# A fixed instruction order on three engines for the attention block of the second mixer

## The chip, the cores and the metric

The kernel runs on one core of a Trainium2 chip. The metric is the device time of one execution in microseconds (us), as a median over runs. The core's engines work side by side, each through its own list of instructions in order: PE (TensorE: matrix products and transposes), DVE (VectorE), ACT (ScalarE), POOL (GpSimd) and SP (SyncE, which issues the transfers). An instruction that needs the result of another engine waits for a semaphore, and everything behind it on its own engine waits with it.

## The reference, cut to what matters

The reference is one step of a two-layer trunk for 128 prompt tokens and 256 latent tokens of width 1024: in each layer a half SwiGLU, a mixer, and a half SwiGLU. The mixer of layer 1 holds two attentions with 8 heads of 64 each: a sliding window with a sink (SWA), and a two-dimensional neighbourhood with a relative bias (NA). The outputs of both are concatenated and multiplied by one weight matrix:

```python
def odd_mixer_latent(h, params, cache):
    w_in, w_out, rpb, sink = params
    kc_ctx, vc_ctx, kd_ctx, vd_ctx = cache
    L = h.shape[1]
    qc, kc, vc, qd, kd, vd = odd_project(h, w_in)
    yc = na_latent(qc, kc, vc, kc_ctx.astype(kc.dtype), vc_ctx.astype(vc.dtype), rpb)
    cos, sin = axial_rope(L, qd.dtype)
    yd = swa_latent(apply_rope(qd, cos, sin), apply_rope(kd, cos, sin), vd,
                    kd_ctx.astype(kd.dtype), vd_ctx.astype(vd.dtype), sink)
    return jnp.concatenate([yc, yd], axis=-1) @ w_out, ()
...
    # in both, for each block of 128 queries:
    p = jax.nn.softmax(scores, axis=-1)      # SWA: a sink column, a band mask; NA: scores + bias
    o = p @ v
```

## The kernel before, in words

**Two halves of each number.** Every product with a weight is made of three matmuls on halves of both factors: `whi` and `wlo` are the rounded weight and what rounding left of it (`hh`, `hl` and `ydh`, `ydl` are the same for activations). ACT rounds (`whi`, line 121), and DVE or POOL subtracts (`wlo`, line 122). A transfer brings a block `raw`; in the attention block all of `wlo` is POOL's (`ws.every = 1`).

**The attention block** (`mixer1`, lines 1135 to 1155) has 24 items: 8 pairs of heads, four of SWA and then four of NA, and for each pair three blocks T of 128 tokens in the order T = 1, 2, 0. T = 1 and 2 are latent tokens (384 keys, two turned tiles), and T = 0 is the prompt (128 keys, one turned tile). For an item, PE makes the scores `S` of both heads (lines 658 and 659, with a mask in SWA, line 707), DVE writes the sink column (709) or adds the bias (711) and takes the maximum (628), ACT makes the exponentials `E` (630), DVE takes the reciprocal of their sum (631) and scales `E` (633), PE transposes `E` into `pt` (719), ACT copies it to `PT` (723, 725), PE multiplies it with the values (732), ACT rounds the result (`ydh`, `ych`, 637) and DVE subtracts (`ydl`, `ycl`, 638). The tile `pt` has two banks. A T = 1 or 2 item takes both, and the value product writes into the first, so the next item's transposes wait for the `ydl` of the one before.

**The turn of item n** is, in the program: its transposes; some fill; the scores and probabilities of item n+2; its value products and split; some more fill. A fill is a unit of three weight matmuls of a list with 64 units: the queries of the four NA pairs (`fm`, after which ACT and DVE make the stack `qn`, lines 647 and 648), then the output product of SWA (`mo`). `FILL = ((1, 2), (1, 2), (0, 1))` says how many units come at the two places for n mod 3. "Slot" below is a place at which a new block of weights is split, which falls into a fill about every 3.5 turns.

**The key stacks of NA** (`na_keys`, for each pair two half-stacks of 64 rows by 512): ACT rounds (`kdn`, 653), POOL copies the rounded half to the other partitions (1103), DVE subtracts (`kln`, 655).

**What sets the order.** Only PE is bound to the program's order there (`in_order`). ACT and DVE take their order from the framework's scheduler, which moves instructions by its own model; POOL and SP too.

Of the kernel before, what the change touches and what calls it, by code (L numbers as in the profile page):

```python
# [13 lines left out]
P = 128  # L14
# [122 lines left out]
def body(ctx, tc, d):  # L137
# [483 lines left out]

    def soft(pool, S, n, nk):

        nm = pool.tile([P, 2], F32, tag="nm", name="nm", bufs=3)
        sm = pool.tile([P, 2], F32, tag="sm", name="sm", bufs=3)
        E = work(pool, 2 * n, "E", 770, 2).rearrange("p (a n) -> p a n", a=2)
        for j in range(2):
            nc.vector.tensor_reduce(nm[:, j:j + 1], S[j][:, :n], axis=AX.X, op=ALU.max, negate=True)
        for j in range(2):
            nc.scalar.activation(E[:, j], S[j][:, :n], AF.Exp, bias=nm[:, j:j + 1], accum_out=sm[:, j:j + 1])  # L630
        nc.vector.reciprocal(sm, sm)
        for j in range(2):
            nc.vector.tensor_scalar(E[:, j, :nk], E[:, j, :nk], sm[:, j:j + 1], None, op0=ALU.mult)
        return E

# [7 lines left out]

    def stack_q(q, p, j):
# [16 lines left out]
    class Stacks:  # L661
# [20 lines left out]
        def keys(self, src, T):  # L682
# [12 lines left out]
    def attn(pool, i, T, scores, vals, Y, mask=None, sink=None, bias=None):  # L695

        nb = len(vals)
        nk = nb * P
        st = {}

        def probabilities():
            S = [bank("S", "S") for _ in range(2)]
            for j in range(2):
                scores(S[j], i, j, T, mask is not None and T > 0)
                if mask is not None and T > 0:
                    o = P if T == 2 else 2 * P
                    nc.tensor.matmul(S[j][:, o:o + P], identb, mask[:, T - 1], start=False, stop=True)
                if sink is not None:
                    nc.vector.tensor_copy(S[j][:, nk:nk + 1], sink(i, j))
                if bias is not None and T > 0:  # L710
                    nc.vector.tensor_tensor(S[j][:, 0:2 * P], S[j][:, 0:2 * P], bias(T)[:, j], op=ALU.add)
            st["E"] = soft(pool, S, nk + (sink is not None), nk)

        def turned():
            pt = [bank("pt", "pt") for _ in range(1 + (nb > 1))]
            for j in range(2):
                for k in range(nb):
                    o = (k if nb > 1 else j) * P
                    nc.tensor.transpose(pt[j * (nb > 1)][:, o:o + P], st["E"][:, j, k * P:(k + 1) * P], ident)  # L719
            PT = st["PT"] = work(pool, 2 * nk, "PT", 768, 1).rearrange("p (a n) -> p a n", a=2)  # L720
# [5 lines left out]
            st["y"] = pt[0][:, NT:NT + P]  # L726

        def output():
            y, PT = st["y"], st["PT"]
            for k in range(nb):  # L730
                for j in range(2):
                    nc.tensor.matmul(y[64 * j:64 * j + 64, :], vals[k](j), PT[:, j, k * P:(k + 1) * P],  # L732
                                     start=k == 0, stop=k == nb - 1)
            split_y(y, Y[i][0][:, T * P:(T + 1) * P], Y[i][1][:, T * P:(T + 1) * P])

        return probabilities, turned, output
# [3 lines left out]
    def finish(left=0):  # L740

        while len(tails) > left:
            for step in tails.pop(0):
                step()

    def attn_pair(pool, i, scores, vf, vctx, Y, mask=None, sink=None, bias=None):
        for T in (1, 2):
            vals = [lambda j: vf(j, 1), lambda j: vf(j, 2)]
            yield attn(pool, i, T, scores, vals + [vctx] if bias else [vctx] + vals, Y, mask, sink, bias)
        yield attn(pool, i, 0, scores, [lambda j: vf(j, 0)], Y, None, sink)  # L750
# [25 lines left out]
    def mixer0():  # L776
        with ExitStack() as es:
# [135 lines left out]
            def attn_a(i):  # L913
                for first, *rest in attn_pair(mp, i, sk.scores, vf, lambda j: vctx[:, 64 * j:64 * j + 64], YA):
                    first()
                    tails.append(rest)
# [134 lines left out]
    def mixer1():  # L1051
        with ExitStack() as es:
# [45 lines left out]
            def na_keys(i):  # L1098
                rpb = mp.tile([P, 2, 2, 256], F32, tag="rpb", name="rpb", bufs=2)
                nc.sync.dma_start(rpb, d["rpb"][:, i])  # L1100
                kl, kd = kln[i % 2], mp.tile([P, 2, 512], F32R, tag="kdn", name="kdn", bufs=2)
                for j in range(2):
                    stack_k(kd[:, j], kl[:, j], kc[:, i], j, lambda d, s: nc.gpsimd.tensor_copy(d, s))
                kn[i] = kd, kl, rpb
# [30 lines left out]
            items = [it for i in range(4) for it in swa(i)] + [it for i in range(4) for it in na(i)]  # L1135
            ws.every = 1
# [207 lines left out]
```

## Time and profile before

| | us |
|---|---|
| median of 3 runs | 1545.02 (1544.58 to 1545.17) |
| the profiled execution | 1544.98 |
| its span in the trace | 1543.3 |
| mean granted clock of PE | 0.993 of full speed |
| PE busy | 1507.2, 98% of the span |
| DVE busy | 1130.4, 73% |
| ACT busy | 681.2, 44% |
| POOL busy | 138.8, 9% |
| attention block, 1139.10 to 1237.34 | 98.24, of which PE busy 90.11 |

Busy times overlap, so they do not add up to the span. A row of a timeline gives the start in us from the span's start, the duration, the engine, the line, the operation and what it writes and reads; a bracket at its end says how long the engine had idled and on whom it waited. Neighbours that are alike are joined into one row (x2), whose duration then runs from the first one's start to the last one's end.

### The profile page before, as it was taken

To read this page: it belongs to the slowest core of one execution; us is meant where nothing else is said; L and a number is where in the kernel's file an instruction comes from. 1 tells how busy PE (TensorE), PEld (TensorE's weight loads), DVE (VectorE), ACT (ScalarE), POOL (GpSimd) and SP (SyncE) were. 2 spreads that over 40 slices of the span, in tenths; PEclk is the share of its full clock that TensorE was granted. 3 is DMA by queue.
4 is the path that set the end of the run, shared out by engine and by line. 5 is a ranking of instruction groups with operands and counts; after the bars stand their busy time and mean duration, and the time that the engine had idled before them with its cause. 6 is when DMAs were issued, how large, how long until landed. Compare 5 with 4: busy or idle time off the path is not lost.

```text
span 1543.3 us, 23024 instructions
## 1 busy us (share of the span) xinstructions
PE 1507.2 (98%) x8888; PEld 1450.6 (94%) x8888; DVE 1130.4 (73%) x2158; ACT 681.2 (44%) x1318; POOL 138.8 (9%) x120
## 2 busy tenths in 40 slices
PE   7999999998999999999999999999999999999997
PEld 5999999996888999999999999999887799999997
DVE  3799999976666899999449899954857777444333
ACT  4643333366654643333345433333667555333321
POOL 2100000113011200000000000001222220000010
PEclk9999999999999999999999999999999999999999
DMA  9555666543002546666354566634431223333331
GB/s 379 225 191 215 249 252 238 213 145 111 28 28 96 217 149 255 235 235 218 112 209 172 214 229 263 240 118 155 143 120 42 69 101 119 137 110 137 119 127 41
DMA packets 40654, 256.91 MB, mean 166 GB/s; under 512 B 4448, under 2 KB 8544, under 8 KB 11232
## 3 DMA queue, kind: packets, MB, share of 16 engines
q1 hardware_dynamic: 40544, 255.43, 46.0%
q8 instruction: 70, 1.15, 0.3%
q14 instruction: 40, 0.33, 0.1%
HBM read 252.52 MB, written 2.89 MB: 166 GB/s over the span
## 4 chain that ended last, share of the span: by engine, by line
PE 94%; DVE 3%; issue 1%; ACT 1%; DMA 0%; POOL 0%; POOLq 0%; SPq 0%; DVEq 0%; ACTq 0%
PE gu L378 16%; PE gu L379 16%; PE gu L380 16%; PE fo L380 8%; PE fo L378 8%; PE fo L379 8%; PE tm L589 2%; PE tm L590 2%; PE pt L732 2%; PE tm L591 2%; PE mo L378 2%; PE mo L380 1%; PE mo L379 1%; PE pt L719 1%; PE fm L378 1%
## 5 line engine op out<-in xcount | busy, mean ns | idle before, releaser
L121 ACT ACTIVATE whi<-raw 128x1024 fp32r<-128x1024 f32 (+2 forms) x378 | 344.6, 927 | 630.5 <-issue 204.7
L122 DVE TENSOR_TENSOR wlo<-raw,whi 128x1024 fp32r<-128x1024 f32 (+2 forms) x335 | 372.4, 1118 | 195.9 <-ACT whi L121 194.7
L378 PE MATMUL gu<-mh,whi 128*128 128x384 f32 x976 | 329.1, 338 | 1.4 <-ACT whi L121 1.4
L379 PE MATMUL gu<-ml,whi 128*128 128x384 f32 x976 | 329.0, 337 | 0.0
L380 PE MATMUL gu<-mh,wlo 128*128 128x384 f32 x976 | 328.2, 337 | 0.0
L256 DVE SCALAR_TENSOR_TENSOR junk<-adaw,cond 128x1024 bf16<-128x1024 f32 x256 | 313.1, 1223 | 2.1 <-DMA adaw<-ada 0.4
L378 PE MATMUL fo<-gh,whi 128*128 128x384 f32 x704 | 235.1, 334 | 0.0
L379 PE MATMUL fo<-gl,whi 128*128 128x384 f32 x704 | 235.1, 334 | 0.0
L380 PE MATMUL fo<-gh,wlo 128*128 128x384 f32 x704 | 235.1, 334 | 0.0
L378 PEld LDWEIGHTS gu<-mh,whi 128*128 128x128 f32 x976 | 183.8, 188 | 2.3 <-ACT whi L121 2.3
L380 PEld LDWEIGHTS gu<-mh,wlo 128*128 128x128 f32 x976 | 183.7, 188 | 0.0
L379 PEld LDWEIGHTS gu<-ml,whi 128*128 128x128 f32 x976 | 183.6, 188 | 0.0
L378 PE MATMUL gu<-hh,whi 128*128 128x386 f32 x432 | 149.4, 346 | 1.4 <-ACT hh L350 1.4
L379 PE MATMUL gu<-hl,whi 128*128 128x386 f32 x432 | 147.1, 341 | 1.5 <-DVE hl L351 1.5
L380 PE MATMUL gu<-hh,wlo 128*128 128x386 f32 x432 | 146.2, 340 | 0.0
L292 POOL TENSOR_TENSOR ssq<-ssq,sq 128x384 f32<-128x384 f32 x43 | 49.0, 1139 | 1055.7 <-issue 798.1
L378 PEld LDWEIGHTS fo<-gh,whi 128*128 128x128 f32 x704 | 132.1, 188 | 0.0
L379 PEld LDWEIGHTS fo<-gl,whi 128*128 128x128 f32 x704 | 132.1, 188 | 0.0
L380 PEld LDWEIGHTS fo<-gh,wlo 128*128 128x128 f32 x704 | 132.1, 188 | 0.0
L378 PEld LDWEIGHTS gu<-hh,whi 128*128 128x128 f32 x432 | 81.8, 189 | 4.8 <-issue 2.9
L379 PEld LDWEIGHTS gu<-hl,whi 128*128 128x128 f32 x432 | 81.8, 189 | 2.1 <-DVE hl L351 2.1
L380 PEld LDWEIGHTS gu<-hh,wlo 128*128 128x128 f32 x432 | 81.8, 190 | 0.0
(286 smaller groups left out, 2069.2 us busy)
## 6 DMA issues: line engine op xcount, KB each, us to landing
adaw<-ada SPq DMA_DIRECT2D x64, 1024.0 KB, 5.4
raw<-f2i SPq DMA_DIRECT2D x44, 1024.0 KB, 4.7
raw<-f1i SPq DMA_DIRECT2D x43, 1024.0 KB, 4.8
raw<-f1o SPq DMA_DIRECT2D x22, 1024.0 KB, 4.8
raw<-f2o SPq DMA_DIRECT2D x22, 1024.0 KB, 4.7
raw<-mo SPq DMA_DIRECT2D x8, 1024.0 KB, 4.9
aw<-aw SPq DMA_DIRECT2D x7, 1024.0 KB, 7.7
raw<-mic SPq DMA_DIRECT2D x6, 1024.0 KB, 4.8
```

The costliest lines, as they stand in the source:

```text
L121: i1 = nc.scalar.activation(hi[:, a:e], src[:, a:e], AF.Copy)
L122: i2 = (self.nc.gpsimd if j % self.every == 0 else self.sub).tensor_tensor(lo[:, a:e], src[:, a:e], hi[:, a:e].bitcast(F32), op=ALU.subtract)
L256: iv = nc.vector.scalar_tensor_tensor(junk, t, 1.0, ada_state["cond"][:, g], op0=ALU.mult, op1=ALU.mult, accum_out=MOD[l][:, j, g, c:c + 1])
L292: nc.gpsimd.tensor_tensor(ssq_t["t"], ssq_t["t"], sq, op=ALU.add)
L378: nc.tensor.matmul(out, wh, xh, start=first, stop=False)
L379: nc.tensor.matmul(out, wh, xl, start=False, stop=False)
L380: return nc.tensor.matmul(out, wl, xh, start=False, stop=last)
L589: nc.tensor.matmul(out[T], hh, wh, start=k == 0, stop=False)
L590: nc.tensor.matmul(out[T], hh, wl, start=False, stop=False)
L591: nc.tensor.matmul(out[T], hl, wh, start=False, stop=k == DC - 1)
L719: nc.tensor.transpose(pt[j * (nb > 1)][:, o:o + P], st["E"][:, j, k * P:(k + 1) * P], ident)
L732: nc.tensor.matmul(y[64 * j:64 * j + 64, :], vals[k](j), PT[:, j, k * P:(k + 1) * P], start=k == 0, stop=k == nb - 1)
```

## The change

The closure `attn` becomes a class `Item` with the steps `scores`, `exps`, `scaled`, `turned`, `values` and `split`, and the block binds ACT and DVE to the program's order too. A turn is now: transposes; fill; scores of n+2 (both heads' products, then both masks, then for each head sink or bias and maximum); value products of n; exponential of n+2's head 0; split of n; exponential of head 1; fill; reciprocal and scaling of n+2; and in eight named turns one half-stack of NA keys. The half-stack's subtraction goes from DVE to POOL, and its rounding for the first two pairs from ACT to DVE. The first mixer uses the same class with its steps in the old order.

```diff
-    def stack_k(kd, kl, k, j, dup):
+    def stack_k(kd, kl, k, j, dup, sub, rounded=None):
         b, o = halves(j)
-        nc.scalar.activation(kd[b], k[b], AF.Copy)
+        (rounded or copy)(kd[b], k[b])
         dup(kd[o], kd[b].bitcast(F32))
-        nc.vector.tensor_tensor(kl[b], k[b], kd[b].bitcast(F32), op=ALU.subtract)
+        sub.tensor_tensor(kl[b], k[b], kd[b].bitcast(F32), op=ALU.subtract)
...
+        def scores(self):
+            S = self.S = [bank("S", "S") for _ in range(2)]
             for j in range(2):
-                scores(S[j], i, j, T, mask is not None and T > 0)
-                if mask is not None and T > 0:
-                    o = P if T == 2 else 2 * P
-                    nc.tensor.matmul(S[j][:, o:o + P], identb, mask[:, T - 1], start=False, stop=True)
...
+                self.products(S[j], self.i, j, self.T, self.mask is not None)
+            if self.mask is not None:
+                o = P if self.T == 2 else 2 * P
+                for j in range(2):
+                    nc.tensor.matmul(S[j][:, o:o + P], identb, self.mask[:, self.T - 1], start=False, stop=True)
...
+        def exps(self, *heads):
+            for j in heads:
+                nc.scalar.activation(self.E[:, j], self.S[j][:, :self.n], AF.Exp, bias=self.nm[:, j:j + 1],
+                                     accum_out=self.sm[:, j:j + 1])
+
+        def scaled(self):
+            nc.vector.reciprocal(self.sm, self.sm)
+            for j in range(2):
+                nc.vector.tensor_scalar(self.E[:, j, :self.nk], self.E[:, j, :self.nk], self.sm[:, j:j + 1], None, op0=ALU.mult)
...
-            def na_keys(i):
...
+            def na_keys(i, j):
...
+                stack_k(kd[:, j], kl[:, j], kc[:, i], j, nc.gpsimd.tensor_copy, nc.gpsimd, nc.vector.tensor_copy if i < 2 else copy)
...
+            keys = {5: (0, 0), 6: (0, 1), 8: (1, 0), 9: (1, 1), 12: (2, 0), 13: (2, 1), 15: (3, 0), 16: (3, 1)}
             ws.every = 1
-            with in_order(tc, (nc.tensor.engine,)):
+            with in_order(tc, (nc.tensor.engine, nc.scalar.engine, nc.vector.engine)):
...
-                for n, (_, turned, output) in enumerate(items):
-                    if n in (6, 8):
-                        na_keys(n // 2 - 3)
-                    turned()
+                for n, it in enumerate(items):
+                    new = items[n + 2] if n + 2 < len(items) else None
+                    it.turned()
                     fill(FILL[n % 3][0])
-                    if n + 2 < len(items):
-                        items[n + 2][0]()
-                        if n + 2 > 12 and (n + 2) % 3 == 2 and n < 18:
-                            na_keys((n + 2) // 3 - 2)
-                    output()
+                    if new:
+                        new.scores()
+                    it.values()
+                    if new:
+                        new.exps(0)
+                    it.split()
+                    if new:
+                        new.exps(1)
                     fill(FILL[n % 3][1])
+                    if new:
+                        new.scaled()
+                    if n in keys:
+                        na_keys(*keys[n])
```

ACT's list at the slot of turn n = 7, whose item is the T = 2 block of the third SWA pair. Before:

```order
L723 ACTIVATE PT<-pt 128x384 x2
L121 ACTIVATE whi_11453<-raw_10951 128x512 x2
L647 ACTIVATE qn<-fm 64x384
L630 ACTIVATE E,sm<-S,nm 128x385
L637 ACTIVATE ydh_10885<-pt 128x128
L630 ACTIVATE E,sm<-S,nm 128x385
L350 ACTIVATE hh_12179<-mod_90 128x2
L647 ACTIVATE qn<-fm 64x384
L350 ACTIVATE hh_12205<-mod_90 128x2
L725 ACTIVATE PT<-pt 128x256
```

The same place of the change:

```order
L734 ACTIVATE PT<-pt 128x384 x2
L716 ACTIVATE E,sm<-S,nm 128x385
L623 ACTIVATE ydh_10885<-pt 128x128
L350 ACTIVATE hh_12179<-mod_90 128x2
L716 ACTIVATE E,sm<-S,nm 128x385
L636 ACTIVATE qn<-fm 64x384
L350 ACTIVATE hh_12205<-mod_90 128x2
L636 ACTIVATE qn<-fm 64x384
L121 ACTIVATE whi_11450<-raw_10951 128x512 x2
L736 ACTIVATE PT<-pt 128x256
```

The two `whi`, after which POOL makes its two `wlo`, stood ahead of the exponentials, and now stand behind both of them and behind both `qn`, right before the `PT` copy of the T = 0 item.

DVE's list at the same turn, after the change; `RECIPROCAL` and the two `TENSOR_SCALAR` that scale `E` stand behind both halves of `qn`, and the sink columns and maxima of the next item come right after them.

```order
L624 TENSOR_TENSOR ydl_10886<-pt,ydh_10885 128x128
L351 TENSOR_TENSOR hl_12180<-mod_90,hh_12179 128x2
L637 SCALAR_TENSOR_TENSOR qn<-fm,qn 64x384
L351 TENSOR_TENSOR hl_12206<-mod_90,hh_12205 128x2
L637 SCALAR_TENSOR_TENSOR qn<-fm,qn 64x384
L720 RECIPROCAL sm<-sm 128x2
L722 TENSOR_SCALAR E<-E,sm 128x384 x2
L708 COPY S<-m1v 128x1
L711 TENSOR_REDUCE nm<-S 128x1
```

So on DVE everything of the next item now stands behind a scaling that comes after `qn`.

POOL's list over the block. Before, four copies of half-stacks come at once ahead of the block, and the others in pairs; before:

```order
L122 TENSOR_TENSOR wlo_11276<-raw_10951,whi_11275 128x512 x2
L122 TENSOR_TENSOR wlo_11454<-raw_10951,whi_11453 128x512 x2
L122 TENSOR_TENSOR wlo_11604<-raw_11006,whi_11603 128x512 x2
L1103 CAST kdn<-kdn 64x512 x2
L122 TENSOR_TENSOR wlo_11775<-raw_11006,whi_11774 128x512 x2
```

After:

```order
L122 TENSOR_TENSOR wlo_11276<-raw_10951,whi_11275 128x512 x2
L643 CAST kdn<-kdn 64x512
L644 TENSOR_TENSOR kln_10607<-kc,kdn 64x512
L643 CAST kdn<-kdn 64x512
L644 TENSOR_TENSOR kln_10607<-kc,kdn 64x512
L122 TENSOR_TENSOR wlo_11451<-raw_10951,whi_11450 128x512 x2
L643 CAST kdn<-kdn 64x512
L644 TENSOR_TENSOR kln_10608<-kc,kdn 64x512
```

Each half-stack's copy and subtraction now stand between the `wlo` of two slots, one half-stack at a time.

## Rows read from the trace of the kernel before

**Rows 1.** Page, busy time of each engine.

```profile
PE 1507.2 (98%) x8888; PEld 1450.6 (94%) x8888; DVE 1130.4 (73%) x2158; ACT 681.2 (44%) x1318; POOL 138.8 (9%) x120
```

**Rows 2.** Seven stretches from one T = 2 transposes to the next: us, PE, PEld, DVE, ACT, POOL, clock.

```profile
1148.94:1159.32 10.38, 10.34 (x81) 8.63 (x79) 7.13 (x26) 7.51 (x24) 2.53 (x2) 1.00 0.29 102
1159.32:1169.91 10.59, 10.59 (x80) 8.87 (x79) 7.37 (x27) 7.92 (x24) 2.52 (x2) 1.00 0.01 2
1169.91:1180.71 10.80, 10.69 (x81) 8.69 (x80) 8.18 (x32) 8.55 (x29) 2.52 (x2) 1.00 0.30 99
1180.71:1193.23 12.52, 10.05 (x76) 8.30 (x75) 9.40 (x28) 9.20 (x28) 3.65 (x4) 1.00 0.13 42
1193.23:1208.36 15.13, 11.58 (x77) 9.66 (x76) 12.15 (x31) 8.53 (x27) 5.07 (x5) 0.89 0.32 105
1208.36:1218.83 10.47, 10.07 (x77) 8.54 (x75) 8.28 (x28) 6.85 (x22) 2.52 (x2) 1.00 0.00 1
1218.83:1229.53 10.70, 9.96 (x76) 8.29 (x75) 7.49 (x24) 7.08 (x22) 1.61 (x2) 1.00 0.01 2
```

**Rows 3.** Waits of PE in the block: us in total, times, longest us.

```profile
PE pt L719 <- DVE ycl L638: 3.7, 4, 1.8
PE pt L732 <- ACT PT L725: 1.8, 2, 1.1
```

**Rows 4.** Timeline of PE, ACT and DVE over a T = 0 turn.

```profile
1152.78 0.58 ACT L630 ACTIVATE E<-S,nm 128x385 f32<-128x385 f32 x1 [0.35 <-DVE nm L628]
1154.77 0.28 ACT L637 ACTIVATE ydh<-pt 128x128 fp32r<-128x128 f32 x1 [0.84 <-PE pt L732]
1154.55 1.02 DVE L628 TENSOR_REDUCE nm<-S 128x1 f32<-128x385 f32 x2
1155.49 0.28 DVE L638 TENSOR_TENSOR ydl<-pt,ydh 128x128 fp32r<-128x128 f32 x1
1155.29 1.08 PE L719 MATMUL pt<-kst,E 128*128 128x128 f32 x6
```

**Rows 5.** The chain that ended last, at that turn's scores: start, us.

```profile
1153.63 0.18 PE S L659
1153.81 0.07 PE S L707
```

**Rows 6.** Timeline of ACT and DVE at the first and second slots.

```profile
1148.06 0.36 ACT L630 ACTIVATE E<-S,nm 128x129 f32<-128x129 f32 x1
1150.74 0.16 DVE L709 COPY S<-m1v 128x1 f32<-128x1 f32 x1 [0.20 <-PE S L707]
1159.39 1.15 ACT L121 ACTIVATE whi<-raw 128x512 fp32r<-128x512 f32 x2
1160.45 0.47 ACT L647 ACTIVATE qn<-fm 64x384 fp32r<-64x384 f32 x1
1160.95 0.55 DVE L648 SCALAR_TENSOR_TENSOR qn<-fm,qn 64x384 fp32r<-64x384 f32 x1 [0.99 <-ACT qn L647]
1164.08 0.75 DVE L633 TENSOR_SCALAR E<-E,sm 128x384 f32<-128x384 f32 x2
```

**Rows 7.** Timeline of POOL and DVE at the fifth slot.

```profile
1199.45 2.62 POOL L122 TENSOR_TENSOR wlo<-raw,whi 128x512 fp32r<-128x512 f32 x2 [5.34 <-ACT whi L121]
1200.01 2.27 DVE L633 TENSOR_SCALAR E<-E,sm 128x384 f32<-128x384 f32 x2
```

**Rows 8.** Timeline of ACT, DVE and POOL at the third pair's key stacks.

```profile
1191.27 1.28 ACT L653 ACTIVATE kdn<-kc 64x512 fp32r<-64x512 f32 x2 [0.32 <-PE S L658]
1191.93 1.71 DVE L655 TENSOR_TENSOR kln<-kc,kdn 64x512 fp32r<-64x512 f32 x2 [0.26 <-ACT kdn L653]
1192.03 2.08 POOL L1103 CAST kdn<-kdn 64x512 fp32r<-64x512 f32 x2 [4.47 <-ACT kdn L653]
1205.70 2.10 DVE L655 TENSOR_TENSOR kln<-kc,kdn 64x512 fp32r<-64x512 f32 x2
```

**Rows 9.** A stretch of the projection ahead of the block; columns as in group 2.

```profile
1099.00:1102.00 3.00, 3.00 (x14) 2.42 (x14) 2.94 (x5) 2.92 (x8) 2.18 (x3) 1.00 0.00 0
```

More of the change, by code (lines that the diff above doesn't have):

```diff
@@ L620, in rope @@
         return u[:, :n]
[L622 to L634, printed above, removed]
     def split_y(y, hh, hl):
@@ L642, in halves, with copy @@
         return slice(64 * j, 64 * j + 64), slice(64 - 64 * j, 128 - 64 * j)
+    def copy(d, s):
+        nc.scalar.activation(d, s, AF.Copy)
     def stack_q(q, p, j):
@@ L725, in turned, with values, split @@
                 nc.scalar.activation(PT.rearrange("p a n -> p (a n)"), pt[0][:, :2 * P], AF.Copy)
[L726 to L730, printed above, removed]
+            self.y = pt[0][:, NT:NT + P]
+        def values(self):
+            for k in range(self.nb):
                 for j in range(2):
[L732 to L736, printed above, removed]
+                    nc.tensor.matmul(self.y[64 * j:64 * j + 64, :], self.vals[k](j), self.PT[:, j, k * P:(k + 1) * P],
+                                     start=k == 0, stop=k == self.nb - 1)
+        def split(self):
+            split_y(self.y, *self.Y)
     tails = []
@@ L748, in attn_pair @@
             vals = [lambda j: vf(j, 1), lambda j: vf(j, 2)]
-            yield attn(pool, i, T, scores, vals + [vctx] if bias else [vctx] + vals, Y, mask, sink, bias)
-        yield attn(pool, i, 0, scores, [lambda j: vf(j, 0)], Y, None, sink)
+            yield Item(pool, i, T, scores, vals + [vctx] if bias else [vctx] + vals, Y, mask, sink, bias)
+        yield Item(pool, i, 0, scores, [lambda j: vf(j, 0)], Y, None, sink)
     def mix_out(l, Y, last, nxt=None):
@@ L913, in attn_a @@
             def attn_a(i):
-                for first, *rest in attn_pair(mp, i, sk.scores, vf, lambda j: vctx[:, 64 * j:64 * j + 64], YA):
-                    first()
-                    tails.append(rest)
+                for it in attn_pair(mp, i, sk.scores, vf, lambda j: vctx[:, 64 * j:64 * j + 64], YA):
+                    it.scores()
+                    it.exps(0, 1)
+                    it.scaled()
+                    tails.append(it)
                     finish(1)
@@ L1096, in swa @@
                                  lambda j: vdc[:, 64 * j:64 * j + 64], YD, mask=maskb, sink=lambda i, j: sinkv[:, i + 4 * j:i + 4 * j + 1])
-            def na_keys(i):
[L1099 to L1104, printed above, removed]
+            def na_keys(i, j):
+                if j == 0:
+                    rpb = mp.tile([P, 2, 2, 256], F32, tag="rpb", name="rpb", bufs=2)
+                    nc.sync.dma_start(rpb, d["rpb"][:, i])
+                    kn[i] = mp.tile([P, 2, 512], F32R, tag="kdn", name="kdn", bufs=2), kln[i % 2], rpb
+                kd, kl, _ = kn[i]
+                stack_k(kd[:, j], kl[:, j], kc[:, i], j, nc.gpsimd.tensor_copy, nc.gpsimd, nc.vector.tensor_copy if i < 2 else copy)
             def na(i):
```

48 lines of the change are left out of this document (30 added, 18 removed).

## The prediction

> **What bounds the kernel now.** I read the page first: PE is busy for 1507.2 of a span of 1543.3 us [rows 1], so a change of order can only win where PE waits. Then I cut the attention block into stretches, from the transposes of one T = 2 item to those of the next pair's [rows 2]. Each of the seven holds three turns and the same PE work but for masks (three pairs of heads have them, four have not) and chance gaps in the records. The reader is to see that five stretches last 10.4 to 10.8 us, two last 12.52 and 15.13, and that PE idles mainly in those two: their sum of 80.59 holds 73.28 of PE work, so 7.3 is idle, and (12.52 - 10.05) + (15.13 - 11.58) = 6.0 of that lies in the two. They are those that hold key stacks. The waits of PE [rows 3] name the culprits: the subtraction `ycl` of DVE that frees the banks (3.7 in four waits, one of 1.8), and the copy `PT` of ACT (1.8 in two). In the fifth stretch the granted clock is 0.89 on average, not 1.00: after PE had waited, part of that stretch ran at the lower level of 1.2 GHz. (1 - 0.89) x 15.13 = 1.7 us went that way.
>
> **What the change removes.** (1) The key subtractions leave DVE. A pair of them stands there for 1.71 [rows 8] and another for 2.10, and both are queued ahead of a `ycl` or a scaling. In their place DVE gets four roundings of one half-stack, all in the SWA turns. The trace has no such operation on DVE; it is bounded by nothing (hidden) and by half of the 1.28 of ACT's pair [rows 8], 0.64 each. I take nothing, since DVE then idles until the next item's scores come. POOL needs half of 2.08 for a copy and, by its own `wlo` of twice the partitions, not over half of 2.62 for a subtraction [rows 7, 8], which the key turns, over 3 us apart, hold. (2) The stacks that the scheduler had put ahead of the block go into it. PE was full where they stood, 3.00 of 3.00 [rows 9], so leaving that place gains nothing. (3) The collision at the fifth slot goes. There POOL's pair of `wlo` ran from 1199.45 for 2.62, and the two scalings that began at 1200.01 took 2.27 in place of 0.75 as at 1164.08 [rows 6, 7]: each ended just behind one of POOL's operations. All this was in the two long stretches, which without it are like their neighbours, 10.5 to 10.7.
>
> **What the change adds, turn by turn.** (4) In a T = 0 turn, ACT rounded `ydh` as soon as the products ended (1154.77), and then took the exponential of 0.58 [rows 4]. Now the exponential of head 0 stands ahead: the first maximum is there at 1154.55 + 1.02 / 2 = 1155.06, so it ends at 1155.64, `ydh` at 1155.92 and `ydl`, 0.28 on, at 1156.2; before, `ydl` ended at 1155.77 because DVE was in the maxima until 1155.57. So 0.45 to 0.5 later, and it is what the next transposes wait for: six of them took 1.08 [rows 4], where they need some 0.82, with a stall in the middle. The two copies `PT` of the next turn now come one behind the other, which I count at 0.15 to 0.2 won back. Net 0.3 a stretch in SWA: from the mean of the first three, (10.38 + 10.59 + 10.80) / 3 = 10.59, to 10.9. NA has no masks and its undisturbed stretches are 10.47 and 10.70 [rows 2]; I take 10.7.
>
> (5) Masks behind both heads: head 0's maximum waits for two more products at 0.18 [rows 5], 0.35 us. In a turn DVE is busy then; at the start of the block nothing covers it: +0.35 once.
>
> (6) The slots. In the old order of turn 7 the two `whi` came ahead of the exponentials, so POOL's pair lay beside the maxima. Now they come behind the exponential of head 1 and both `qn`. From that exponential's end: ACT needs 2 x 0.47 for `qn` and then half of 1.15 for the first `whi` [rows 6], so POOL starts its 2.52 [rows 2] at 1.5 and ends at 4.1. DVE makes the second `qn` until 0.94 + 0.55 = 1.5, takes the reciprocal, and starts to scale at 1.7, in the middle of POOL's first: as at the fifth slot [rows 7], it is through some 0.1 behind POOL, at 4.2. Uncovered it would be 1.7 + 0.75 = 2.5. Behind it on DVE stand the sink, the maxima and the `ydl` of the next turn, and behind these maxima, on ACT, the exponential that now precedes `ydh`; so PE's next transposes wait for all of it. When are those maxima due? If the next item is T = 0 (turns 7 and 10): the exponential ended at 1153.36 and the first mask now ends at about 1153.81 + 2 x 0.18 + 0.07 = 1154.24 [rows 4, 5], 0.9 later; I take 1.0. If it is T = 1 (turn 0): the exponential ended at 1148.42, the sink was written at 1150.74 and now 0.35 later [rows 6], 2.7 on.
> - Turn 0: 4.2 - 2.7 = +1.5.
> - Turns 7 and 10: 4.2 - 1.0 = 3.2, of which PE has one fill unit, three matmuls or 0.5, and some slack of the split to cover it: +2.5 each. Bounds 1.5 (2.5 - 1.0, if POOL's work does not hold up the scaling) and 3.2.
> - Turn 4, where the weights fall into the first fill and `qn` and `whi` stand ahead of the exponentials: 1.15 more on ACT there, half covered, +0.6.
> - Turn 14, without `qn`: the second scaling is begun before POOL is. Between nothing and 2.52 / 2 = 1.3 I take 0.65. The key roundings that ACT keeps, 0.64 each, stand ahead of a `PT` copy in turns 13 and 16: +0.4 each. Those of 12 and 15 have more room and cost nothing.
>
> **The sum.** Stretches by forecast: 10.9 + 1.5 = 12.4; 10.9 + 0.6 = 11.5; 10.9 + 2.5 = 13.4; 10.9 + 2.5 = 13.4 (still partly SWA); 10.7 + 0.65 + 0.4 = 11.75; 10.7 + 0.4 = 11.1; 10.7. Together 84.25, against 80.59: +3.7. With the start +4.0. On the profiled execution of 1544.98 that is 1549.0; the median of before is only 0.04 from it. So some 6 us of stalls go, and nearly 10 come in other places.
>
> Of the collision, the Trainium skill says on its page "SBUF — State Buffer", section "Who interferes with whom", that VectorE and GpSimd share one pair of ports as an exclusive lock: an operation of the `tensor_scalar` kind may run in a mode that takes the pair, and then whoever comes second blocks for the other's whole instruction. The 2.27 in place of 0.75 [rows 7] agrees. By that rule the changed order puts scaling and `wlo` onto one another; if only the usual 0.75 held, the sum would be the one of case B below.
>
> **The rivals.**
> - **A, collisions at the slots (above): 1549.0.** For it speaks the row of 2.27, and that order now places `whi` right ahead of the scaling. Against it, that it is seen clearly only once before.
> - **B, DVE is through before POOL or not held up by it: 1544.8.** Turn 0 costs nothing (2.5 under 2.7), turns 7 and 10 cost 1.5 each, turn 14 nothing: 10.9 + 11.5 + 12.4 + 12.4 + 11.1 + 11.1 + 10.7 = 80.1, -0.5, with the start -0.15: 1544.8, no change.
> - **C, the other side: turns absorb the slots, 1540.4.** PE has its next item's transposes and fills ahead, two items deep; if the lateness of a scaling is made up within the two turns until `E` is turned, every stretch is 10.8: 75.6, -5.0, with the start -4.6: 1540.4. For it speaks that three stretches with slots lost no more than 0.3 [rows 2] before. It decides where DVE's maxima can slip by over 2 us without a transpose waiting; the wait of 1.8 on `ycl` [rows 3] speaks against.
> - **D, slower still: 1552.3.** Two waits of over 2 us, as in A, each lower the clock as in the fifth stretch, 1.7 each: +3.4.
>
> **Chances.** A 0.42, B 0.24, C 0.22, D 0.12. What a measurement can tell from no change is 0.2%, 3.1 us. Faster than 1541.9 is C without its dull end: 0.21. Within, B and the mild part of A (bound 1.5 for turns 7 and 10, which gives 1547.0), with the rest of C: 0.36. Slower than 1548.1: 0.43. The range goes from just inside C to D: 1541.0 to 1552.5. A alone would be 1546.5 to 1551.5.
>
> **What would show it.** In the trace after: (1) no `kln` on DVE and both long stretches near 11; (3, 6) scalings of over 1.5 us for a pair beside POOL's `wlo` in turns 0, 7 and 10, and stretches 1, 3 and 4 of over 12; waits of PE for `ydl` there; (4) `ydh` behind an exponential in T = 0 turns, with the transposes behind it over 1.3; (5) the block's first transposes 0.35 later. I am wrong if the scalings last 0.75 and stretches 3 and 4 stay under 11.5, or if the clock falls in them.

## The result, and the profile after

The changed kernel takes 1560.18 us (median of 4, 1559.66 to 1560.62), against 1545.1 of before in the same session: a ratio of 1.0088, 95% interval 1.0076 to 1.0101. It is slower, and lies above the range of the forecast (1541.0 to 1552.5). The profiled execution took 1559.82, its span is 1557.6, 14.3 over that of before.

The seven stretches of the changed kernel, cut as in [rows 2] from one T = 2 transposes to the next, with the same columns:

```profile
1149.81:1162.93 13.12, 10.59 (x80) 8.81 (x79) 10.22 (x28) 7.70 (x24) 2.49 (x2) 1.00 0.21 80
1162.93:1175.06 12.13, 10.12 (x80) 8.61 (x79) 8.11 (x28) 7.80 (x24) 4.17 (x4) 1.00 0.01 2
1175.06:1191.45 16.39, 12.42 (x81) 10.63 (x79) 11.30 (x33) 8.72 (x29) 6.57 (x7) 0.79 0.19 65
1191.45:1210.34 18.89, 13.60 (x77) 11.47 (x76) 13.47 (x31) 9.17 (x28) 5.14 (x6) 0.73 0.09 28
1210.34:1222.09 11.75, 10.30 (x77) 8.56 (x75) 10.21 (x27) 8.13 (x24) 5.88 (x5) 1.00 0.14 46
1222.09:1233.00 10.91, 9.85 (x76) 8.36 (x75) 8.44 (x26) 7.78 (x24) 5.46 (x6) 1.00 0.28 97
1233.00:1244.00 11.00, 9.79 (x76) 8.37 (x75) 8.95 (x26) 6.54 (x21) 0.95 (x1) 1.00 0.01 2
```

Their sum is 94.19, 13.6 over the 80.59 of before, and the first T = 2 transposes come 0.87 later than before. So the loss is in the block. In the seven stretches PE is busy for 76.68 against 73.28 with the same work, because the granted clock is 0.79 and 0.73 in the third and fourth, and idle for 17.5 against 7.3. That is 10.2 more of waits, and 3.4 more of busy time; the clock itself costs more than these 3.4, since before had lost some of it too (0.89 in its fifth stretch). The 0.87 ahead of them is made of two waits of PE:

```profile
1144.78 0.85 PE L731 MATMUL pt<-kst,E 128*128 128x128 f32 x6 [1.12 <-DVE E L722]
1147.48 0.71 PE L742 MATMUL pt<-PT,m1v 128*64 128x128 f32 x3 [0.93 <-ACT PT L734]
```

Before waited 0.64 at the first place and not at all at the second; the block's first product starts at 1138.59, 0.51 earlier than before, which takes back a part. The waits of PE from 1140 to 1260, which holds all of the block but its first 1.4 us:

```profile
PE pt L742 <- ACT PT L736: 8.3, 6, 3.5
PE pt L731 <- DVE ydl L624: 5.7, 4, 1.8
PE pt L731 <- DVE ycl L624: 2.3, 3, 1.2
PE pt L742 <- ACT PT L734: 2.1, 3, 0.9
PE pt L731 <- DVE E L722: 1.1, 1, 1.1
```

Against [rows 3] the first line is new in size: 8.3 us for the copy `PT` of T = 0 items, where before had 1.8. Where it arises, on all four engines at the slot of turn 7 (timeline; the bracket says what ended the idle time ahead):

```profile
1179.46 0.47 ACT L636 ACTIVATE qn<-fm 64x384 fp32r<-64x384 f32 x1
1180.55 0.48 ACT L636 ACTIVATE qn<-fm 64x384 fp32r<-64x384 f32 x1 [0.53 <-DVE qn L637]
1181.06 1.15 ACT L121 ACTIVATE whi<-raw 128x512 fp32r<-128x512 f32 x2
1182.23 0.38 ACT L736 ACTIVATE PT<-pt 128x256 f32<-128x256 f32 x1
1185.41 0.58 ACT L716 ACTIVATE E<-S,nm 128x385 f32<-128x385 f32 x1 [2.80 <-DVE S L708]
...
1181.84 2.82 DVE L722 TENSOR_SCALAR E<-E,sm 128x384 f32<-128x384 f32 x2
...
1181.82 2.62 POOL L122 TENSOR_TENSOR wlo<-raw,whi 128x512 fp32r<-128x512 f32 x2 [3.79 <-issue]
...
1182.67 0.44 PE L742 MATMUL pt<-PT,kvd 128*64 128x128 f32 x4 [2.35 <-ACT PT L736]
1186.63 0.90 PE L731 MATMUL pt<-kst,E 128*128 128x128 f32 x3 [1.63 <-DVE ydl L624]
```

Three things are to be seen. On ACT, the two `qn`, a gap of 0.53 between them in which ACT waits for DVE's half of the first, and the two `whi` stand for 2.75 us ahead of `PT`, and PE waits 2.35 for it. On DVE the two scalings take 2.82 beside POOL's `wlo`, the next item's maxima come behind them, ACT's exponential waits 2.80 for these, and the `ydh` behind it makes PE wait again, 1.63. And the transposes at 1186.63 take 0.90 for three, where three of them behind such a wait take 0.55 at full clock (1159.56): PE runs at the lower of its two levels, 1.2 GHz, by then. The stretch in pieces, columns as above:

```profile
1175.00:1180.00 5.00, 5.00 (x41) 4.38 (x39) 2.72 (x10) 2.81 (x10) 2.15 (x3) 1.00 0.00 0
1180.00:1185.00 5.00, 2.65 (x14) 1.78 (x12) 4.53 (x8) 2.04 (x5) 2.62 (x2) 0.80 0.00 2
1185.00:1190.00 5.00, 3.37 (x21) 3.25 (x22) 3.47 (x14) 3.03 (x11) 1.58 (x2) 0.51 0.62 210
1190.00:1195.00 5.00, 5.00 (x43) 4.38 (x40) 3.92 (x10) 2.04 (x8) 2.18 (x3) 1.00 0.01 3
```

The granted clock falls behind the wait of 2.35 and is back at 1.00 from 1190 on, after PE has worked without a wait since 1186.63. The slot of turn 10 shows the same with 3.48 and 1.81. The four waits add up to 9.27, all of the idle time of the two stretches: 16.39 - 12.42 + 18.89 - 13.60 = 9.26.

### The profile page after: what moved, and what is told of

Same layout as the page of the kernel before. It is cut to its first block, busy times and chain, and to the rows that moved or that the text cites. A ratio compares the mean times of both kernels' runs of the same rounds, so it can differ in the third digit from the quotient of the medians.

```text
span 1557.6 us, 23025 instructions
## 1 busy us (share of the span) xinstructions
PE 1511.3 (97%) x8888; PEld 1455.1 (93%) x8888; DVE 1137.7 (73%) x2154; ACT 679.2 (44%) x1314; POOL 147.4 (9%) x128
## 4 chain that ended last, share of the span: by engine, by line
PE 93%; DVE 3%; ACT 2%; issue 1%; DMA 0%; POOL 0%; POOLq 0%; SPq 0%; DVEq 0%; ACTq 0%
PE gu L378 16%; PE gu L379 16%; PE gu L380 16%; PE fo L378 8%; PE fo L379 8%; PE fo L380 8%; PE tm L589 2%; PE tm L590 2%; PE tm L591 2%; PE mo L378 1%; PE mo L380 1%; PE mo L379 1%; PE pt L742 1%; PE pt L731 1%; PE fm L378 1%
```

## The experiments

Three suspects stood at the start: **L**, the scaling held up by POOL's `wlo` (the forecast's own); **P**, `qn` and `whi` ahead of the `PT` copy in ACT's bound list; **X**, the exponential that now stands ahead of `ydh`. A fourth came out of the runs: **H**, the hand-over between ACT and DVE inside `qn`. A fifth suspect got no run of its own: DVE's tiny `hl` of 128x2, which POOL's subtractions hold up as they do the scaling (last section). Each run is the changed kernel with the edit shown; the interval behind a ratio to before is of 95%. "Sum" is that of the seven stretches in the profiled execution, which lies up to 3.3 us from the median (e6 and e14 above it, e13 below).

| run | median | ratio | sum |
|---|---|---|---|
| before | 1545.1 | 1 | 80.59 |
| the change | 1560.18 | 1.0088 (1.0076 to 1.0101) | 94.19 |
| e1 only PE bound | 1549.11 | 1.0022 (1.0013 to 1.0032) | 79.83 |
| e2 scaling first | 1555.16 | 1.0064 (1.0047 to 1.0080) | 90.45 |
| e3 `wlo` on DVE | 1560.66 | 1.0100 (1.0085 to 1.0115) | 95.15 |
| e4 `qn` behind `PT` | 1559.87 | 1.0095 (1.0080 to 1.0110) | 94.54 |
| e5 split first | 1556.59 | 1.0072 (1.0057 to 1.0087) | 91.46 |
| e6 split and scaling first | 1553.21 | 1.0047 (1.0031 to 1.0064) | 89.97 |
| e7 ACT free | 1554.72 | 1.0060 (1.0045 to 1.0075) | 91.62 |
| e8 DVE free | 1558.46 | 1.0081 (1.0066 to 1.0096) | 90.76 |
| e9 slots a turn later | 1560.36 | 1.0096 (1.0081 to 1.0111) | 94.43 |
| e10 e9 with e6 | 1560.45 | 1.0097 (1.0082 to 1.0112) | 94.37 |
| e11 ACT free, scaling first | 1559.28 | 1.0085 (1.0069 to 1.0102) | 96.18 |
| e12 only PE bound, early keys as before | 1547.15 | 1.0007 (0.9998 to 1.0016) | 82.25 |
| e13 no hand-over | 1558.42 | 1.0084 (1.0066 to 1.0103) | 91.29 |
| e14 no hand-over, scaling first | 1552.65 | 1.0050 (1.0035 to 1.0065) | 89.90 |
| e15 e14 and split first | 1548.78 | 1.0019 (1.0010 to 1.0029) | 82.79 |
| e16 e15, `whi` a turn later | 1550.87 | 1.0035 (1.0022 to 1.0047) | 85.27 |
| e17 e15, `whi` behind `PT` | 1550.35 | 1.0030 (1.0018 to 1.0041) | 84.34 |
| e18 e17, masks by head | 1549.28 | 1.0022 (1.0013 to 1.0032) | 85.17 |

### Whose bound order costs: e1, e7, e8

```diff
-with in_order(tc, (nc.tensor.engine, nc.scalar.engine, nc.vector.engine)):
+with in_order(tc, (nc.tensor.engine,)):                      # e1
+with in_order(tc, (nc.tensor.engine, nc.vector.engine)):     # e7
+with in_order(tc, (nc.tensor.engine, nc.scalar.engine)):     # e8
```

> The changed kernel, with only TensorE bound to the program's order; the framework's scheduler again places ACT's and DVE's work, from the new steps, keys and masks. If the pinned order of ACT and DVE is what costs (both theories below): the two stretches of 16.4 and 18.9 us go back to 10.5 to 12.5, time 1543 to 1548. If the moved key subtraction, the masks or the new steps themselves cost: 1555 or more.

> The changed kernel with TensorE and VectorE bound to the program's order and ScalarE left to the scheduler. Theory P (ACT's pinned list, qn and whi ahead of the PT copy): the PT waits of 2.35 and 3.48 go, 6 us and part of the clock: 1549 to 1553. If DVE's list alone sets the time (theory L with the maxima behind the scaling): 1557 to 1561.

> The changed kernel with TensorE and ScalarE bound and VectorE left to the scheduler. Theory L (scaling behind qn, blocked by POOL, with the next maxima behind it): if the scheduler puts the scaling ahead of qn or the maxima ahead of the scaling, the ydl waits go and it is near scaling first, 1552 to 1556. If ACT's list alone sets the time: 1558 to 1561.

With only PE bound, the sum is 79.83: the new steps, masks and keys cost nothing in the loop, and the bound order of ACT and DVE costs all of the 14 us there. Freeing one of the two gives back 2.6 (ACT) and 3.4 (DVE) of the sum, 5.5 and 1.7 of the median. What each list holds can be seen in the waits of the third and fourth stretch. With ACT free (e7) those on the T = 0 copy `PT` fall from 2.35 and 3.48 to none and 1.10, and DVE's stay (0.89 and 0.98 on `E`, 1.39 and 1.90 on `ydl`). With DVE free (e8) those on `ydl` go, and `PT` stays at 2.86 and 3.70. So each list has a chain of its own. The rest of e1's excess lies ahead of the block, where the scheduler again puts early key stacks. There DVE now rounds them and POOL subtracts. The 20 us of the projection in e1, and in before (columns as in [rows 2]):

```profile
1100.00:1120.00 20.00, 17.42 (x92) 13.86 (x91) 19.53 (x28) 8.35 (x18) 10.61 (x10) 1.00 0.35 118
```

```profile
1100.00:1120.00 20.00, 19.43 (x114) 16.72 (x113) 18.84 (x35) 12.23 (x26) 5.03 (x5) 1.00 0.35 119
```

PE loses 2.0 us there that it did not lose before, 0.53 and 1.49 of it in waits for DVE's `hl`.

### The keys: e12

```diff
-  stack_k(..., nc.gpsimd.tensor_copy, nc.gpsimd, nc.vector.tensor_copy if i < 2 else copy)
+  stack_k(..., nc.gpsimd.tensor_copy, nc.vector if i < 2 else nc.gpsimd)
```

(with PE alone bound, as in e1)

> Only TensorE bound, and the first two pairs' key stacks rounded on ACT and subtracted on DVE as before (those of the last two pairs subtracted on POOL). The scheduler puts the first ones into the projection. If the 2.6 us of PE's waits there (1100 to 1120 us, on DVE's hl, in the run with TensorE alone bound) come from roundings on DVE and subtractions on POOL that lock each other: they go, 1545.5 to 1547, and with the last two pairs' subtraction off DVE at most 1 us better than before: 1544 to 1546.5. If they come from the scheduler's other placing: 1548 to 1550.

1547.15, ratio 1.0007: no change from before, and the projection's loss is gone (PE 19.43 of the same 20 us, as before). The last two pairs' subtraction is off DVE here, and no time is won: PE's waits in turns 11 to 15 read 1.10, 0.72, 0.64, 0.65 and 1.81 in e12, and 1.10, 0.73, 0.63, 1.08, 0.66 and 1.81 in before. One wait of 1.08 went, and in this execution the clock takes more than that back (0.79 and 0.87 in the fourth and fifth stretch, which together last 29.3 against 27.7). The collision [rows 7] is still there, 2.27 for the two scalings, with the wait of 1.81 behind it. So the key subtraction held one wait of 1.08, and the rest of what made the two stretches long is something else.

### The scaling and POOL: e2, e3

```diff
+                    if new:
+                        new.scaled()
                     fill(FILL[n % 3][1])
-                    if new:
-                        new.scaled()
```

> The changed kernel with reciprocal and scaling ahead of the turn's second fill, so ahead of qn on DVE; ACT's and PE's lists stay as they are. Theory L (the scaling blocked by POOL's wlo is the cause): no scaling over 0.5 us each in turns 0, 7 and 10, the waits of PE on ydl of 1.1 to 1.8 go, stretches 1, 3 and 4 lose 1.5 to 2 us each and their clock recovers in part: 1548 to 1553. Theory P (qn and whi ahead of the PT copy on ACT is the cause): ACT's second qn waits for DVE's first, which is now 0.9 later, so the waits on PT grow from 2.35 and 3.48 by up to 0.9: 1560 to 1563.

e3 sets `ws.every = 1 << 30` in the block, so that DVE makes `wlo`.

> The changed kernel with the block's wlo subtractions on DVE instead of POOL. Theory L: the scaling pair is never longer than 0.9 us beside wlo, DVE has 1.2 us more in each of seven slots but 2 us less of blocking in three: 1555 to 1559, PE's ydl waits shorter. If the lock plays no part, DVE only gets 7 x 1.2 us more: 1561 to 1566. Theory P: the waits on PT stay as they are, 2.3 and 3.5, since ACT's list is the same.

e2 gains 5.0, less than theory L had named (7 to 12): no scaling of it takes over 0.94, and the waits on `ydl` in turns 9 and 12 fall from 1.63 and 1.81 to none. The wait on `PT` in turn 8 grows from 2.35 to 2.96, as theory P had it, and that of turn 11 stays (3.44). L is real, then, and P's wait stands beside it. In e3, with `wlo` on DVE, the scalings behind the slots of turns 0, 7 and 10 take 0.49, 0.75 and 0.75, so it is POOL's `wlo` that holds them in the changed kernel; but no time is won, because DVE has to make `wlo` ahead of the scaling, at the very place where it waited for POOL (`ydl` 1.73 and 1.97).

### Moving qn and the slots: e4, e9, e10, e11

e4 puts ACT's and DVE's `qn` behind the next turn's transposes. e9 collects `qn`, `whi` and `wlo` of the turns n mod 3 = 1 and issues them a turn later:

```diff
+                    if n % 3 == 1:
+                        ws.later = []
                     fill(FILL[n % 3][0])
...
+                    if n % 3 == 2:
+                        for step in ws.later:
+                            step()
+                        ws.later = None
```

> The changed kernel with both steps of qn (ACT and DVE) put behind the next turn's transposes and PT copies, so the PT copy of turns 8 and 11 stands behind whi alone, and the scaling does not stand behind qn. Theory P: the waits of 2.35 and 3.48 on PT fall by 1.1 (0.5 and 0.6 for the two qn with ACT's wait between them) to about 1.2 and 2.4. Theory L too: the scaling is begun 0.3 us after the exponential, before POOL's first wlo, so 0.5 to 1.0 us for the pair. Together, and with the clock: 1546 to 1551. If only P holds, about 1557; if neither, 1560.

> The changed kernel, all three lists bound, with the slots of turns n mod 3 = 1 (qn on ACT and DVE, whi and wlo) one turn later, behind the exponentials and the scaling of the T = 0 turn: in turns 7 and 10 neither stands ahead of a scaling or of a T = 0 PT copy. If the slots' place in two turns is what costs (L and P together at turns 7 and 10), the PT waits of 2.35 and 3.48 fall under 1, the ydl waits of 1.6 and 1.8 fall to the 1.1 of the other T = 0 turns, the clock stays up, and stretches 3 and 4 fall from 16.4 and 18.9 to 12 to 13: 1547 to 1551. If being bound in order costs everywhere, no more than 4 us are won: 1556 or more.

> As the run of slots a turn later, with the split ahead of the exponentials and the scaling ahead of the fill as well. If the three act apart, the remaining collision (turn 0), the 1.1 us on ydl in T = 0 turns go too, stretches 10.6 to 11.9: 1541 to 1545, faster than both kernels. If the waits only move, it is no better than slots a turn later alone, 1547 to 1551.

> TensorE and VectorE bound, ScalarE left to the scheduler, and the scaling ahead of the second fill: both chains are opened without moving the slots in the program. If L and P add: 1554.7 of ScalarE free less the 5.0 of scaling first: 1548 to 1551. If each only hands its wait to the other: 1553 to 1555.

None of the four was faster than the change by more than the noise, and e10 and e11 lie above both of the outcomes named for them. In each, one wait went and another came. In e4 the waits on `PT` fall to 0.69 and 0.73, as P says, but those on `ydl` rise to 3.07 and 2.82: ACT's `qn` now stand behind `whi` and `PT` (the first at 1183.77), on DVE an `hl` takes 0.96 beside POOL's `wlo` just ahead of its half, ACT's second half waits 0.97 for that, and DVE's maxima stand behind all of it. In e10 the `PT` waits go from turns 8 and 11 to turns 6, 9 and 12 with 2.8 each. ACT's list of e10 at turn 5 shows why:

```profile
1169.52 0.47 ACT L643 ACTIVATE qn<-fm 64x384 fp32r<-64x384 f32 x1
1171.23 0.49 ACT L643 ACTIVATE qn<-fm 64x384 fp32r<-64x384 f32 x1 [1.23 <-DVE qn L644]
1171.74 1.15 ACT L123 ACTIVATE whi<-raw 128x512 fp32r<-128x512 f32 x2
1172.91 0.87 ACT L741 ACTIVATE PT<-pt 128x384 f32<-128x384 f32 x2
```

Two operations of 0.5 take 2.2 us, because ACT's second waits for DVE's first, and DVE now scales before that. The same place in before, where the scheduler put two `PT` copies into the gap:

```profile
1160.45 0.47 ACT L647 ACTIVATE qn<-fm 64x384 fp32r<-64x384 f32 x1
1160.82 0.85 ACT L723 ACTIVATE PT<-pt 128x384 f32<-128x384 f32 x2
1161.69 0.49 ACT L647 ACTIVATE qn<-fm 64x384 fp32r<-64x384 f32 x1
```

That is H. It explains a part of e11 as well, where the scheduler orders ACT by itself: DVE scales first, ACT's second `qn` comes at 1182.29 after 0.56 of waiting, DVE's second only behind it, the maxima behind that, and PE waits 3.12 and 3.60 for `ydl`. More than the 0.56 was lost ahead of that scaling: the scheduler had put `whi` early, POOL's `wlo` ran from 1178.49 to 1181.01, and beside it two `hl` of DVE took 0.68 and 1.23, where each takes 0.15 alone.

### The split: e5, e6

```diff
+                    it.split()
                     if new:
-                        new.exps(0)
-                    it.split()
-                    if new:
-                        new.exps(1)
+                        new.exps(0, 1)
```

> The changed kernel with the split of item n ahead of both exponentials of item n+2 (on ACT ydh no longer stands behind an exponential that waits for DVE's maxima; the PE list is the same). Theory X (the exponential ahead of ydh carries DVE's lateness into the transposes): the ydl waits of 1.14, 1.14, 1.63, 1.81 fall to under 0.6 each and the clock recovers in the two slow stretches: 1550 to 1555. If the ydl waits come from DVE's own list (ydl stands behind the maxima, and these behind the blocked scaling), they fall by no more than the exponential's 0.58 each: 1557 to 1560. The waits on PT (2.35, 3.48) stay in both.

> The changed kernel with both: scaling ahead of the second fill, and the split ahead of the exponentials. If the two act apart, the gains add: below the 1555.2 of scaling first alone by what the split first alone gains, 1550 to 1553, with only the PT waits (3.0 and 3.4) left. If the split first helps only where the scaling is late, it adds under 1.5: 1554 to 1555.

X is worth 0.3 to 0.4 where no slot is near: the waits on `ydl` in turns 3 and 6 fall from 1.14 to 0.75 and 0.82, those of turns 9 and 12 do not (1.90 and 2.74). The median falls by 3.6, and with scaling first by 2.0 (the intervals of e2 and e6 overlap).

### Without the hand-over: e13 to e18

e13 issues both of ACT's `qn` and then both of DVE's; ACT's second then waits for DVE no longer: in e15 the two start at 1190.44 and 1190.93 and take 0.98 together, where the changed kernel needed 1.57.

```diff
-                    for j in range(2):
-                        stack_q(qn[i][:, j], p[:, :NT], j)
+                    nc.scalar.activation(q[b, 0], f[b], AF.Copy, scale=0.125)
+                    nc.scalar.activation(q[c, 1], f[c], AF.Copy, scale=0.125)
+                    nc.vector.scalar_tensor_tensor(q[o, 0], f[b], 0.125, q[b, 0].bitcast(F32), op0=ALU.mult, op1=ALU.subtract)
+                    nc.vector.scalar_tensor_tensor(q[e, 1], f[c], 0.125, q[c, 1].bitcast(F32), op0=ALU.mult, op1=ALU.subtract)
```

> The changed kernel with both of ACT's qn ahead of both of DVE's, so that ACT's second no longer waits for DVE's first; nothing else moves. Theory H (the hand-over is a main part of ACT's lateness at the slots): ACT is 0.53, 0.62 earlier with whi and PT in turns 8 and 11, POOL starts its wlo as much earlier, DVE's scaling too, so each of the three slots with qn behind the exponentials is 0.5 to 0.7 shorter, with the clock 2 to 4 us: 1556 to 1558. If the hand-over is hidden behind POOL's wlo and the scaling: no change, 1559.5 to 1560.5.

> As e13, and the scaling ahead of the fill. With scaling first alone the hand-over was longer (DVE scales before it makes the first qn), and the PT waits were 2.96 and 3.44. Theory H: they fall by the hand-over of 0.9 to 1.2, to about 1.9 and 2.2, and the clock recovers in part: 1549 to 1553. If whi and the two qn themselves (0.94 + 1.15) hold PT, they stay over 2.5: 1554 to 1555.5.

> As e14, and the split ahead of the exponentials. The split ahead took off 2 us beside scaling first (1555.2 to 1553.2). Expected by adding: 1547 to 1551; no more than e14 if the exponentials now lie on PT's path instead (they come 0.3 us later with the split ahead).

e13 alone: the `PT` waits fall from 2.35 and 3.48 to 1.84 and 1.89, but the `ydl` wait of turn 12 rises to 2.81; two of four executions are near 1556 and two near 1561, so its worth by itself is not settled. e14 is 2.5 below e2, with overlapping intervals; its waits on `PT` are 1.84 and 2.48 in place of e2's 2.96 and 3.44, as H had it. e15 is 4.4 below e6, outside the intervals. In e15 the clock holds but for one stretch:

```profile
1150.67:1161.82 11.15, 10.48 (x80) 8.79 (x79) 7.68 (x27) 7.95 (x24) 2.50 (x2) 1.00 0.27 94
1161.82:1173.38 11.56, 10.12 (x80) 8.60 (x79) 7.95 (x28) 8.12 (x24) 3.92 (x4) 1.00 0.01 2
1173.38:1185.69 12.31, 10.11 (x80) 8.60 (x79) 9.58 (x33) 8.27 (x28) 6.25 (x7) 1.00 0.20 69
1185.69:1199.32 13.63, 11.29 (x76) 9.75 (x75) 10.16 (x30) 8.99 (x30) 4.91 (x5) 0.87 0.17 55
```

The third stretch has 10.11 of PE work where the changed kernel had 12.42. So three edits that move nothing on PE give back 11.4 of the 15.1 us. Alone they gave 5.0, 3.6 and 1.8, 10.4 added up (the 1.8 uncertain, see e13): within the noise they add.

e16 and e17 move `whi` and `wlo` as well: a turn later, or behind the `PT` copies of the next T = 1 or 2 turn. e18 is e17 with each mask behind its own head's products again.

> As e15, with whi and wlo of the turns n mod 3 = 1 one turn later, behind the T = 0 turn's exponentials. Then the T = 0 PT copy stands behind two qn alone. If whi is the rest of the PT wait, it falls by 1.15 to under 1 us in turns 8 and 11 and about 0.4 to 0.8 comes in turns 9 and 12; the clock stays up: stretches 10.9 to 12, 1543 to 1547. If lateness only wanders along ACT's list, waits of over 2 us turn up at the PT copies of turns 9 and 12: 1549 to 1553.

> As e15 (no hand-over, scaling and split ahead), with whi and wlo of the slots in a second fill put behind the PT copies of the next T = 1 or T = 2 turn, where ACT waits for PE and POOL's wlo lies beside the maxima, as the scheduler of before had it. If whi is the rest of the PT waits: those of turns 8 and 11 fall by 1.15 to about 0.7 and 1.2, the clock stays up in all stretches, the 1.72 on ycl in turn 21 goes; 82.8 - 3 to 4 us: 79 to 80, 1543 to 1546, no slower than before. If the lateness of qn and the exponentials sets PT: 81.5 to 83, 1547.5 to 1549.

> As e17, with each mask behind its own head's products. The term for it in the prediction was 0.35 us once at the start of the block and nothing later: 0.3 to 0.5 us faster than e17. If head 0's maximum, 0.35 us earlier in eight turns, is on the path there too: 1 to 3 us faster. If the order of the masks is worth nothing: within 0.3.

The `PT` waits of turns 8 and 11 fall in e17 as foreseen, to 0.81 and 1.34 (in e16 to 0.81 and 1.86), and its first stretch is 10.35, as good as before. But the sum is no better, 84.34 against 82.79, and the time lies above both outcomes named for it. POOL's two `wlo` now have a key stack between them, and the second comes to lie on a scaling of turn 9:

```profile
1185.75 1.52 DVE L729 TENSOR_SCALAR E<-E,sm 128x128 f32<-128x128 f32 x2
...
1185.71 1.27 POOL L124 TENSOR_TENSOR wlo<-raw,whi 128x512 fp32r<-128x512 f32 x1
```

That costs DVE little here: in e15, where this scaling took 0.49, two `hl` operations beside POOL's `kln` took 0.62 and a pair of them 0.66, and the next item's first maximum starts 2.66 behind the turn's transposes, in e17 2.84. What takes the gain away is the wait that comes next, rows of PE in e17 and, last, in e15:

```profile
1191.89 0.44 PE L749 MATMUL pt<-PT,kvd 128*64 128x128 f32 x4 [1.34 <-ACT PT L743]
1194.92 0.90 PE L738 MATMUL pt<-kst,E 128*128 128x128 f32 x3 [1.54 <-DVE ydl L631]
...
1193.05 0.44 PE L742 MATMUL pt<-PT,kvd 128*64 128x128 f32 x4 [2.34 <-ACT PT L736]
```

DVE works from 1190.60 to 1194.87 without a gap of note (reciprocal, scaling, both `qn`, two additions of the bias, two maxima, `ydl`), and the same list stands in e15 from 1190.58 to 1194.85. There PE came to the transposes 1.3 later, because it had waited 2.34 for `PT`, and found `ydl` ready; 1.0 less of that wait uncovers 1.54 of this one. The clock is 0.87 and 0.79 in the third and fourth stretches of e17. e18 puts the block's first wait on `E` from 1.12 to 0.64, the 0.64 that before had; beyond that its difference to e17, 1.1, is within the spread of the runs of either. No version with ACT and DVE bound beat the kernel before.

## Why the prediction was wrong, by its own steps

The sign was right, and the collision that the forecast built on is there (e2, e3). But it is one of several chains: e2, which takes it away, gives back 5.0 of the 15.1 us. The step that failed is (6) with rival D: it followed the lateness on DVE alone, gave the T = 0 `PT` copy no term and the clock a small chance. Forecast 1549.0, range to 1552.5.

- **(1) keys off DVE: wrong as a cause of both long stretches.** The last three stretches came as forecast in length (11.75, 10.91 and 11.00 against 11.75, 11.1 and 10.7; that the first agrees to the last digit is chance, its waits are 0.50 and 0.39 on `PT` and 0.56 on `ycl`), so the longest one of before did go. But e12 takes the later subtractions off DVE and wins no time: one wait of 1.08 goes, the others stay, the 1.81 behind the collision [rows 7] among them. I had read the operation that lay in the stretch as the reason for its length. And POOL's subtraction, which I took to cost nothing, held an `hl` of DVE for 1.20 in turn 10 (last section): the first addition of the bias starts at 1194.19, 0.7 behind the scores that it reads (the last of them ran from 1193.16 to 1193.50). The exponentials, `qn`, `whi` and `PT` follow it, so by an estimate from these rows some 0.7 of that slot's 3.48 comes from there.
- **(2) leaving the projection is worth nothing: right.** PE works 19.65 of the 20 us from 1100 in the changed kernel and 19.43 before. The block began 0.51 earlier. The reverse is not free (e1).
- **(4) the exponential ahead of `ydh`: right in place, too small in size.** The forecast had a net 0.3 a stretch. In turns 3 and 6 PE waits 1.14 for `ydl` where it had not waited before; e5 takes off 0.4 and 0.3 of it, and the remaining 0.75 and 0.82 had no term. With waits of 0.57 to 0.86 on `PT` in the same stretches, the first two last 13.12 and 12.13 against 12.4 and 11.5.
- **(5) masks: right**, 0.48 at the block's start against 0.35 (1.12 - 0.64, and e18 gives it back). The 0.93 on `PT` right behind it had no term: DVE's maxima of the second item now stand behind the first item's scaling, both exponentials of that item follow them on ACT, and `PT` stands behind these. e18 still has it (0.94).
- **(6) the slots: right on DVE, and this is where it failed on ACT.** The scaling pairs of turns 0, 7 and 10 take 2.56 (a pair of 128x128, 0.49 elsewhere), 2.82 and 2.81, at the turns and for the reason forecast. Of POOL and VectorE the Trainium skill's page "SBUF — State Buffer" says in "Who interferes with whom" that the engine that issues first has the shared ports for its whole instruction and the other blocks. These rows agree: POOL's `wlo` starts first in all three, by 0.01 to 0.02. For the wait on `ydl` I had 2.5 in each of the two turns; it is 1.63 and 1.81. But I followed only that branch. The order rows of turn 7 showed the T = 0 `PT` copy right behind both `qn` and both `whi`, and no term was given to it: 2.35 + 3.48 = 5.8 us of waits. I had reckoned ACT's two `qn` as 2 x 0.47, though ACT and DVE take the halves in turn and [rows 6] shows DVE's as 0.55: with the hand-over they take 1.57 and 1.57. The same delay sits in the branch that I did follow. DVE begins to scale at turn 7 2.4 behind the end of head 1's exponential, not 1.7, and is through at 5.2, not 4.2. That `ydl` cost less than 2.5 all the same is no merit of the sum: PE came to these transposes 2.35 late from `PT`. By an estimate from the rows, without that wait `ydl` would have cost 2.35 + 1.63 = 4.0; e4, with a `PT` wait of 0.69 and another order on DVE, shows 3.07.
- **Rival D, the clock: it should have been part of the likeliest case.** The forecast gave it 0.12 and 1.7 for each of two stretches, and named a falling clock as a sign that it is wrong. The third and fourth have 12.42 + 13.60 of PE work against 10.69 + 10.05 for the same work at full clock, 5.3. Ahead of it PE had waited 2.35 and 1.63, and 3.48 and 1.81. In the third stretch of e15 it waits 1.85 and 0.35 and the clock stays at 1.00; in that of e17 it waits 0.81 and 0.93 and the clock is 0.87. So the size of a wait alone does not tell what the clock does, and I have no term for it; but what a wait costs here is often not its own length. From e14 to e15 the sum of the profiled executions falls by 7.1, and 5.7 of that is PE's busy time for the same work.

The gap in numbers, third and fourth stretch: forecast 26.8, measured 35.28. PT waits +5.8, clock +5.3, `ydl` waits 3.4 in place of 5.0, and PE work at full clock 10.69 + 10.05 in place of 2 x 10.9: 26.8 + 5.8 + 5.3 - 1.6 - 1.1 = 35.2. That is 8.5 of the 9.9 by which the seven stretches exceed their forecast of 84.25; the first two add 1.35.

What stays open: what a bound order would need to be as good as the scheduler's. Of the waits left in e15, those on `PT` (1.85 and 2.34) became shorter when `whi` was moved and others came for them, and that of 1.72 on `ycl` in turn 21 stayed. Nor did a run take the `hl` operations out of POOL's way.

## What to carry to other kernels

Binding two more engines to the program's order makes each list a chain: for every instruction that moves ahead of another, follow everything behind it on its own engine, and its partners on the others, before pricing it at nothing. A two-step operation that passes between engines for each head (ACT, DVE, ACT, DVE) costs a full round of both when its steps stand together (1.57 us on ACT here, 0.98 without it); issue all of one engine's steps first, or put other work between them. And when a fix only moves a wait, look for the second chain that ends just behind the first: here moving `qn`, `whi` or the slots gave nothing, while three edits that shorten a chain each gave 1.8 to 5.0 alone and 11.4 together.

## What the runs showed of the hardware

A tiny DVE operation with two inputs in SBUF waits for POOL as the scaling does: `hl` of 128x2 takes 0.15 to 0.2, and beside POOL's `kln` in the changed kernel

```profile
1193.07 1.20 DVE L351 TENSOR_TENSOR hl<-mod,hh 128x2 fp32r<-128x2 f32 x1 [0.16 <-ACT hh L350]
...
1192.97 1.28 POOL L644 TENSOR_TENSOR kln<-kc,kdn 64x512 fp32r<-64x512 f32 x1
```

it takes 1.20. The section of the Trainium skill named above ("SBUF — State Buffer", "Who interferes with whom") states this case, two SBUF inputs on VectorE against an instruction of GpSimd that reads SBUF, and the row agrees. DVE's rounding of a half-stack (64x512, SBUF to SBUF) takes 0.41 to 0.42 with POOL idle, against 0.62 to 0.63 on ACT, and POOL's subtraction 1.26 to 1.28, against 0.68 to 1.74 (median 0.99) that DVE had taken.
